# Dilated attention: statistics stored as 16-byte pieces, the softmax over dilations run inside the next pair's first pass, and 160 bytes set aside on the right

## The chip, the cores and the metric

One Trainium2 chip, of which the kernel uses one core. The metric is the device time of one execution in microseconds (us), over runs of the same program; lower is better. Everything is 32-bit floating point: a product that has to be exact is made of three matrix products over operands split into a high and a low part of type fp32r.

## The reference, cut to what matters

Two blocks over 1024 tokens of width 1024. The first runs dilated window attention beside a gated long convolution; the second (a state-space layer and a latent attention) only matters here as the rest of the time. In the first block each of 8 heads attends in three dilation groups (1, 4 and 16), and the three results are weighted by a softmax over the groups' log-denominators:

```python
for g, (window, dilation) in enumerate(DILATED_GROUPS):     # (128,1), (512,4), (2048,16)
    o_g, lse_g = dilated_window_attention(q[g], k[g], v[g], slopes, dilation, radius)
wts = softmax(stack(lses, axis=0), axis=0)
o_attn = einsum('gbsh,gbshe->bshe', wts, stack(outs, axis=0))
y_attn = o_attn.reshape(B, S, D_ATTN) * silu(g_attn)
merged = sigmoid(r_attn) * (y_attn @ w_proj_attn) + sigmoid(r_hy) * (y_hy @ w_proj_hyena)
res = DEEPNORM_ALPHA * x + gate * (merged @ w_out + b_out)
```

## The kernel before

**Who orders the work.** The code is written straight down, and a scheduler that simulates the engines decides in what order each engine takes its instructions; each engine then runs its list in that order and waits on semaphores. DMAs are issued almost all from SP, which also runs its list in order.

**The large products.** `unit()` computes 128 columns of `h @ w_in` and its like for all 1024 tokens. For each of two halves of 512 tokens it runs 8 chunks of the depth times three products on TensorE (L192): weights `wh` with `hh`, `wh` with `hl`, `wl` with `hh`. The 128x128 weight block is the stationary operand, and 512 columns of the activations are the moving one. ACT makes `wh` out of the loaded row (L177), DVE makes `wl` (L182). `hh` and `hl` are the split activations of block 1, in four tiles on the right end of SBUF, each 16 KB in every partition. The last projection of block 1 reads `mh`/`ml`, and block 2 reads `xh`/`xl`, from tiles at the same places. The first projection of the opening stage reads `hh`/`hl` too (L405), the two projections of the block's branches read `yhh`/`yhl` and `yah`/`yal`, the tail reads `xm`. The products of the long convolution (L649) have `yh`/`yl` as their moving operand.

**Where those tiles lie.** In the built program `hh0` begins at byte 196576 of each partition and `hl0` at 212960, `hh1` at 163808, `hl1` at 180192, `mh`/`ml` and `xh`/`xl` at the same numbers. All of these leave a rest of 32 when divided by 64. `yhh` begins at 42816, `yhl` at 51008, `xm0` at 113216, the convolution's `yh` and `yl` at 125760 and 131904, and these leave no rest.

**Attention.** `attention()` runs over four pairs of heads (`hp`) and three groups (`g`). A group's pass takes eight tiles of 128 queries two at a time (`tp` = 0, 2, 4, 6): scores on TensorE (L1103, L1104), bias and row minimum on DVE out of PSUM (L1105), exponential with row sum on ACT (L1108), transposes on TensorE (L1115), their copies to SBUF alternately on DVE (L999) and ACT (L1001), the product with the values (`po`, L1119), and its copies into `og` (L1129 on ACT, L1131 on DVE). Minimum and sum of each query stand in `stat`.

**Between two pairs.** After a pair's third group the statistics go to memory (`stat_d`, L1135 to L1143), two numbers of one head at a time, and come back with tokens on partitions in one DMA (`sn`, L1149). DVE and ACT work out the softmax (`mm` L1156 to `ex` L1167), the weights go out (`w_d`, L1168) and are read back spread over the 64 rows of each head (`w`, L1204), DVE (POOL for g = 1) multiplies them with `og` (L1205), DVE adds (L1207), POOL multiplies with the gate (L1210), and the result goes to memory (L1212). The scheduler moves TensorE work of the next pair, and units of other projections, into that stretch. The last pair has an ending of its own in halves of 512 tokens (L1186 to L1200), after which the merge runs, whose evacuations on DVE are `tg` (L1273).

Of the kernel before, what the change touches and what calls it, by code (L numbers as in the profile page):

```python
# [9 lines left out]
F32 = mybir.dt.float32  # L10
F32R = mybir.dt.float32r
AF = mybir.ActivationFunctionType
ALU = mybir.AluOpType
# [3 lines left out]
P = 128  # L17
S = 1024
# [142 lines left out]
def tile_pool(tc, **kw):  # L161
    return tc.tile_pool(reuse_waits="tile", **kw)
# [147 lines left out]
LAG = 0  # L310


def opening(k, cv):


# [1 line left out]

    nc, tc, A = k.nc, k.tc, k.A
    k.hh, k.hl = [], []
    for h in range(2):  # L320
        p = k.hes.enter_context(tile_pool(tc, name="hT%d" % h, bufs=1, side="right"))
        for n, to in (("hh", k.hh), ("hl", k.hl)):
            to.append(p.tile([P, KD, 512], F32R, name="%s%d" % (n, h)))
    with ExitStack() as es:
# [3 lines left out]
        xp, tp, wp = pool("xp", 8), pool("tp", 2), pool("wada", 3)  # L328
# [4 lines left out]
        xs, rows, ws, mlps = {}, {}, [], []  # L333
# [45 lines left out]
        for h in range(2):  # L379
            for n in range(FIRST):  # L380
                i = h * FIRST + n
# [592 lines left out]
def attention(k):  # L974

    nc, tc, A = k.nc, k.tc, k.A
    k.yaT = [k.dram.tile([4, P, 512], F32, name="yaT%d" % b) for b in range(2)]
    with ExitStack() as es:
# [6 lines left out]
        op = pool("og", 1)  # L985
        gp = pool("gt", 1)
        bp = pool("bias", 1)
        pt_ = pool("ptp", 4)
        st_ = pool("stat", 2)
# [6 lines left out]
        def copy(out, in_):  # L996
# [3 lines left out]
            else:  # L1000
                nc.scalar.copy(out, in_)  # L1001

        for hp in range(4):
            stat_d = k.dram.tile([3, 2, S, 2], F32, name="stat_d%d" % hp)
            w_d = k.dram.tile([3, 2, S], F32, name="w_d%d" % hp)
            og = []
            for g in range(3):
                d = (1, 4, 16)[g]
# [47 lines left out]
                tabs = []  # L1056
                for h in range(2):
                    n = 128 if g == 2 else 256
# [31 lines left out]
                for tp in range(0, 8, 2):  # L1090

                    po = ps_o.tile([P, 2, 2, P], F32, name="po", tag="po")
                    for h in range(2):
                        ps = ps_s.tile([P, 2, 256], F32, name="s%d" % h, tag="s%d" % h)
                        sb = sp.tile([P, 2, 256], F32, name="sb", tag="sb")
                        for m in range(2):
                            t = tp + m
                            a, n, off, z, cs = tiles[t]
                            qt, ks = slice(t * P, (t + 1) * P), slice(a, a + n)
                            for e, rest in ((0, z), (z + n, len(cs) * P - z - n)):  # L1100
                                if rest:
                                    nc.gpsimd.memset(sb[:, m, e : e + rest], 0.0)  # L1102
                            nc.tensor.matmul(ps[:, m, :n], qa[h][:, qt], kh[h][:, ks], start=True, stop=False)  # L1103
                            nc.tensor.matmul(ps[:, m, :n], qa[h][:, qt], kl[h][:, ks], start=False, stop=True)  # L1104
                            nc.vector.tensor_tensor_reduce(sb[:, m, z : z + n], ps[:, m, :n], tabs[h][:, off : off + n],  # L1105
                                                           -0.125, 3.0e38, op0=ALU.add, op1=ALU.min,
                                                           accum_out=stat[:, t, h, 0:1])
                            nc.scalar.activation(sb[:, m, z : z + n], sb[:, m, z : z + n], AF.Exp, scale=-1.0,  # L1108
                                                 bias=stat[:, t, h, 0:1], accum_out=stat[:, t, h, 1:2])
                        nk = len(cs)  # L1110
                        pst = ps_t.tile([P, 4, P], F32, name="pt", tag="pt")
                        pT = pt_.tile([P, 4, P], F32, name="pT", tag="pT")
                        for m in range(2):
                            for x in range(nk):
                                nc.tensor.transpose(pst[:, m * nk + x, :], sb[:, m, x * P : (x + 1) * P], k.idn)  # L1115
                        copy(pT[:, : 2 * nk], pst[:, : 2 * nk])
                        for m in range(2):
                            for x, c in enumerate(tiles[tp + m][4]):
                                nc.tensor.matmul(po[:, h, m, :], vn[:, c, :], pT[:, m * nk + x, :],  # L1119
                                                 start=(x == 0), stop=(x == nk - 1))  # L1120
                    for h in range(2):
                        hs = slice(h * 64, h * 64 + 64)
                        v, to = po[hs, h].rearrange("p m q -> p (m q)"), o[hs, tp * P : (tp + 2) * P]
                        if g:
                            rr = d // 4
                            v = v.rearrange("p (r l) -> p r l", r=rr)
                            to = o[hs].rearrange("p (l r) -> p r l", r=d)[:, tp // 2 * rr : (tp // 2 + 1) * rr]
                        if h:
                            nc.scalar.copy(to, v)  # L1129
                        else:  # L1130
                            nc.vector.tensor_copy(to, v)  # L1131
                for h in range(2):
                    dst = stat_d[g, h]
                    if g == 0:
                        nc.sync.dma_start(dst.rearrange("(t q) c -> q t c", q=P), stat[:, :, h, :])  # L1135
                    elif g == 1:
                        v = dst.rearrange("(i q r) c -> q r i c", q=P, r=4)
                        for r in range(4):
                            nc.sync.dma_start(v[:, r], stat[:, 2 * r : 2 * r + 2, h, :])
                    else:  # L1140
                        v = dst.rearrange("(l t r) c -> r l t c", r=2, t=8)
                        for r in range(2):
                            nc.sync.dma_start(v[r], stat[r * 64 : r * 64 + 64, :, h, :])  # L1143

                if (hp, g) in FILL and late:
                    r_unit(k, late.pop(0), trp)

            sn = st_.tile([P, 3, 2, 8, 2], F32, name="sn", tag="sn")
            nc.sync.dma_start(sn.rearrange("p g h j c -> p (g h) (j c)"),  # L1149
                              stat_d.rearrange("g h (p j) c -> p (g h) (j c)", j=8))  # L1150
            nm = [sn[:, g, :, :, 0] for g in range(3)]
            mm = st_.tile([P, 2, 8], F32, name="mm", tag="mm")
            ex = st_.tile([P, 3, 2, 8], F32, name="ex", tag="ex")
            zz = st_.tile([P, 2, 8], F32, name="zz", tag="zz")
            tz = st_.tile([P, 3, 2, 8], F32, name="tz", tag="tz")
            nc.vector.tensor_tensor(mm, nm[0], nm[1], op=ALU.min)  # L1156
            nc.vector.tensor_tensor(mm, mm, nm[2], op=ALU.min)
            for g in range(3):
                nc.vector.tensor_sub(ex[:, g], nm[g], mm)
            nc.scalar.activation(ex, ex, AF.Exp, scale=-1.0)  # L1160
            for g in range(3):
                nc.vector.tensor_mul(tz[:, g], ex[:, g], sn[:, g, :, :, 1])
            nc.vector.tensor_add(zz, tz[:, 0], tz[:, 1])
            nc.vector.tensor_add(zz, zz, tz[:, 2])
            nc.vector.reciprocal(zz, zz)
            for g in range(3):
                nc.vector.tensor_mul(ex[:, g], ex[:, g], zz)  # L1167
            nc.sync.dma_start(w_d.rearrange("g h (p j) -> p (g h) j", j=8), ex.rearrange("p g h j -> p (g h) j"))  # L1168

            u = UN["g_attn"] + hp  # L1170
            gt = gp.tile([P, S], F32, name="gt", tag="gt")
# [8 lines left out]
            if hp == 3:  # L1180
                for n in late:
                    r_unit(k, n, trp)
            nc.vector.scalar_tensor_tensor(gt, th, 1.0, gt, op0=ALU.add, op1=ALU.mult)
            if hp == 3:

                ws = [gp.tile([P, S], F32, name=n, tag=n) for n in ("wa", "wb")]  # L1186
# [11 lines left out]
                    nc.vector.tensor_mul(gt[:, sl], gt[:, sl], vs[0])  # L1198
                    nc.sync.dma_start(k.yaT[b][hp], gt[:, sl])
                break  # L1200
            for g in range(3):
                w = gp.tile([P, S], F32, name="w", tag="wb" if g else "wa")
                for h in range(2):
                    nc.sync.dma_start(w[h * 64 : h * 64 + 64], w_d[g, h : h + 1, :].to_broadcast([64, S]))  # L1204
                (nc.gpsimd if g == 1 else nc.vector).tensor_mul(w, w, og[g])  # L1205
                if g:
                    nc.vector.tensor_add(acc, acc, w)  # L1207
                else:
                    acc = w
            nc.gpsimd.tensor_mul(gt, gt, acc)  # L1210
            for b in range(2):
                nc.sync.dma_start(k.yaT[b][hp], gt[:, b * 512 : (b + 1) * 512])  # L1212


ON1 = ((0, 2), (0, 1, 2))
# [5 lines left out]
def merge(k):  # L1221
# [5 lines left out]
    def x2half(h):  # L1227
        p = k.x2es.enter_context(tile_pool(tc, name="x2T%d" % h, bufs=1, side="right"))
        k.x2.append([p.tile([P, KD, 512], F32R, name="x%s%d" % (n, h)) for n in "hl"])

    x2half(0)
    with ExitStack() as es, ExitStack() as em:
        def pool(name, bufs, **kw):
# [951 lines left out]
```

## Time and profile before

| | |
|---|---|
| time before, median of 3 runs | 2152.36 us (2147.53 to 2154.57) |
| the profiled execution: its own time, its span | 2153.48 us, 2151.7 us |
| mean granted TensorE clock of the span | 0.974 |
| busy: TensorE, its weight loads, DVE, ACT, POOL | 93%, 77%, 64%, 38%, 20% |
| attention lies at | about 785 to 1290 us of the span |

A row that begins with an engine and a line gives the instructions of that line: output, operands, shape and number. "PE" is TensorE, "PEld" its weight loads, "SPq" SP's issuing of DMAs. In a timeline each row is an instruction or a run of equal ones, with its start, its length, and in square brackets how long the engine stood idle ahead of it and for whom. Successive products of TensorE overlap in such rows; how fast they follow each other is read from their starts. "PEclk" is the granted clock of TensorE as a share of full speed: 1.00 is 2.4 GHz, 0.50 is 1.2 GHz.

### The profile page before, as it was taken

How to read it: one execution, taken by the hardware profiler on the slowest of the kernel's cores; microseconds unless marked ns; L12 is line 12 of the kernel's file. 1: busy time of each engine (PE TensorE's matmuls, PEld its weight loads, DVE VectorE, ACT ScalarE, POOL GpSimd, SP SyncE). 2: the span in 40 equal slices, each digit the busy share in tenths (PEclk: the TensorE clock that was granted, in tenths of full speed). 3: DMA queues.
4: the chain of work that ended last, by engine and by line, in shares of the span. 5: the costliest groups of instructions: out<-in, count | busy, mean ns of one | idle time of the engine just before them, and what ended most of it. 6: DMA issues, size and time to landing. Idle time of an engine off the chain costs nothing. (4 is left out here: it accounts for less than half of the span.)

```text
span 2151.7 us, 29886 instructions
## 1 busy us (share of the span) xinstructions
PE 2006.1 (93%) x10413; PEld 1665.3 (77%) x10413; DVE 1385.3 (64%) x2914; ACT 824.6 (38%) x1659; POOL 430.4 (20%) x448
## 2 busy tenths in 40 slices
PE   4999999999999999799897997999899989999997
PEld 3788878888887888688786875878677777788787
DVE  8987767788786234353434249585876558875685
ACT  3524333333322234444454433243423345554433
POOL 3201210231211001020201002050455233401221
PEclk9999999999999999899998999999899999999999
DMA  8236666766756473546465167363554363436351
GB/s 302 59 119 207 193 207 223 251 211 215 230 193 196 157 200 92 116 99 133 91 138 112 45 178 261 105 203 105 161 145 133 87 184 89 130 117 194 115 178 53
DMA packets 224105, 334.90 MB, mean 156 GB/s; under 512 B 65770, under 2 KB 129936, under 8 KB 223954
## 3 DMA queue, kind: packets, MB, share of 16 engines
q1 hardware_dynamic: 214016, 326.36, 50.6%
q0 software_dynamic: 1952, 4.07, 0.8%
q10 hardware_dynamic: 7986, 2.56, 0.5%
q8 instruction: 83, 1.36, 0.3%
q14 instruction: 68, 0.56, 0.1%
HBM read 251.68 MB, written 80.04 MB: 154 GB/s over the span
## 5 line engine op out<-in xcount | busy, mean ns | idle before, releaser
L192 PE MATMUL pj<-hh,wh 128*128 128x512 f32 x1104 | 441.3, 400 | 3.2 <-DVE kl L1046 2.3
L192 PE MATMUL pj<-hh,wl 128*128 128x512 f32 x1104 | 440.5, 399 | 0.1
L192 PE MATMUL pj<-hl,wh 128*128 128x512 f32 x1104 | 440.4, 399 | 0.0
L177 ACT CAST wh<-raw 128x1024 fp32r<-128x1024 f32 (+3 forms) x196 | 175.0, 897 | 377.5 <-PE pj L192 302.4
L182 DVE TENSOR_TENSOR wl<-raw,wh 128x1024 fp32r<-128x1024 f32 (+2 forms) x177 | 206.1, 1166 | 134.6 <-ACT wh L177 133.9
L192 PEld LDWEIGHTS pj<-hh,wh 128*128 128x128 f32 x1104 | 209.1, 189 | 49.6 <-issue 2.7
L192 PEld LDWEIGHTS pj<-hh,wl 128*128 128x128 f32 x1104 | 209.3, 190 | 45.5 <-DVE wl L182 0.6
L192 PEld LDWEIGHTS pj<-hl,wh 128*128 128x128 f32 x1104 | 209.2, 189 | 44.8
L1108 ACT ACTIVATE sb<-sb,stat 128x192 f32<-128x192 f32 (+2 forms) x192 | 85.5, 447 | 74.7 <-DVE stat L1105 69.4
L1119 PE MATMUL po<-pT,vn 128*128 128x128 f32 x640 | 90.7, 286 | 20.2 <-DVE pT L999 19.8
L1119 PEld LDWEIGHTS po<-pT,vn 128*128 128x128 f32 x640 | 86.1, 200 | 26.2 <-DVE pT L999 21.2
L1105 DVE CUSTOM_DVE_ANT_0 sb<-s,tb 128x192 f32<-128x192 f32 (+2 forms) x192 | 62.2, 344 | 67.9 <-PE s L1104 62.1
L192 PE MATMUL pj<-xh,wl 128*128 128x512 f32 x256 | 104.0, 406 | 1.2 <-DVE wl L182 1.2
L192 PE MATMUL pj<-xh,wh 128*128 128x512 f32 x256 | 103.4, 406 | 0.0
L192 PE MATMUL pj<-xl,wh 128*128 128x512 f32 x256 | 103.3, 404 | 0.0
L1102 POOL MEMSET sb<- 128x64 f32 x80 | 9.8, 152 | 410.3 <-PE pt L1115 364.4
L1131 DVE COPY og<-po 64x256 f32<-64x256 f32 x48 | 26.0, 541 | 86.4 <-PE po L1119 86.1
L1103 PE MATMUL s<-kh,qa 128*128 128x192 f32 (+2 forms) x192 | 60.5, 324 | 16.5 <-DVE stat L1105 15.8
L806 POOL TENSOR_TENSOR zz<-zz,t 128x256 f32<-128x256 f32 x32 | 35.4, 1107 | 182.7 <-DVE t L802 142.2
L1115 PE MATMUL pt<-idn,sb 128*128 128x128 f32 x320 | 63.9, 289 | 3.4 <-ACT sb L1108 2.1
L494 DVE TENSOR_TENSOR bt<-bt 128x256 f32<-128x256 f32 x176 | 63.5, 418 | 0.4
L192 PEld LDWEIGHTS pj<-xh,wl 128*128 128x128 f32 x256 | 48.9, 191 | 13.5 <-DVE wl L182 1.7
(602 smaller groups left out, 4630.4 us busy)
## 6 DMA issues: line engine op xcount, KB each, us to landing
raw<-in_w_in_dram SPq DMA_DIRECT2D x92, 512.0 KB, 3.7
k_fw<-k_fw SPq DMA_DIRECT2D x56, 384.0 KB, 3.8
qkv<-tr SPq DMA_DIRECT2D x80, 256.0 KB, 2.8
raw<-in_w_out_dram SPq DMA_DIRECT2D x32, 512.0 KB, 3.6
k_iv<-k_iv SPq DMA_DIRECT2D x28, 384.0 KB, 4.7
row<-in_w_ada_dram SPq DMA_DIRECT2D x16, 512.0 KB, 6.4
dc<-in_k_decay_dram SPq DMA_DIRECT2D x64, 128.0 KB, 3.5
spec<-sp SPq DMA_DIRECT2D x32, 256.0 KB, 5.3
```

Of the source, the lines that this page charges most:

```text
L177: nc.scalar.copy(hi, src)
L182: (nc.vector if lo_eng == "dve" else nc.gpsimd).tensor_sub(lo, src, f(hi))
L192: nc.tensor.matmul(ps, a, b, start=(i == 0), stop=(i == n - 1))
L494: self.nc.vector.tensor_tensor(out, a, b, op=op)
L806: nc.gpsimd.tensor_sub(zz[:, 0], zz[:, 0], t2[:, 1])
L1102: nc.gpsimd.memset(sb[:, m, e : e + rest], 0.0)
L1103: nc.tensor.matmul(ps[:, m, :n], qa[h][:, qt], kh[h][:, ks], start=True, stop=False)
L1105: nc.vector.tensor_tensor_reduce(sb[:, m, z : z + n], ps[:, m, :n], tabs[h][:, off : off + n], -0.125, 3.0e38, op0=ALU.add, op1=ALU.min, a ...
L1108: nc.scalar.activation(sb[:, m, z : z + n], sb[:, m, z : z + n], AF.Exp, scale=-1.0, bias=stat[:, t, h, 0:1], accum_out=stat[:, t, h, 1:2])
L1115: nc.tensor.transpose(pst[:, m * nk + x, :], sb[:, m, x * P : (x + 1) * P], k.idn)
L1119: nc.tensor.matmul(po[:, h, m, :], vn[:, c, :], pT[:, m * nk + x, :], start=(x == 0), stop=(x == nk - 1))
L1131: nc.vector.tensor_copy(to, v)
```

## The change

Three things are edited.

1. `stat_d` gets a layout with both heads side by side for each token (`[3, S, 2, 2]`), so that a piece written for a query is 16 bytes long where it was 8, and each store carries both heads: 28 stores where there were 56. `sn` then reads pieces of 128 bytes where they were 64.
2. What stood between two pairs becomes a generator, `combined()`, whose steps run inside the next pair's pass over g = 0: the load of `sn` at `tp` = 2; softmax, `w_d` and the loads of two of the three weights at `tp` = 4; the multiplications, the third load, the sums and the stores at `tp` = 6. `issue_after(dve.ins)` and `issue_after(act.ins)` let the scheduler place such a step only behind the last score reduction and the last exponential of that `tp`. The last pair runs the first two steps at once and keeps its own ending.
3. `pad()` takes a tile of 40 numbers (160 bytes) on the right ahead of `hh`/`hl`, and again ahead of `xh`/`xl`. In the built program these tiles, and `mh`/`ml`, begin 160 bytes lower: 196416, 212800, 163648, 180032, which leave no rest when divided by 64. No other moving operand of 512 columns changes its place.

The number of instructions is otherwise the same on each engine.

```diff
+def pad(k, es):
+    es.enter_context(tile_pool(k.tc, name="pad", bufs=1, side="right")).tile([P, 40], F32, name="pad")
...
     k.hh, k.hl = [], []
+    pad(k, k.hes)
...
+        def combined(hp, stat_d, w_d, og):
+            sn = st_.tile([P, 3, 8, 2, 2], F32, name="sn", tag="sn")
+            nc.sync.dma_start(sn.rearrange("p g j h c -> p g (j h c)"),
+                              stat_d.rearrange("g (p j) h c -> p g (j h c)", j=8))
+            yield
...
+            nc.vector.tensor_tensor(mm, nm[0], nm[1], op=ALU.min)
...
+            for g in range(3):
+                nc.vector.tensor_mul(ex[:, g], ex[:, g], zz)
+            nc.sync.dma_start(w_d.rearrange("g h (p j) -> p (g h) j", j=8), ex.rearrange("p g h j -> p (g h) j"))
+            if hp == 3:
+                yield
+            ws = {}
...
+            load(0)
+            load(1)
+            yield
+            for g in range(3):
+                if g == 2:
+                    load(2)
+                (nc.gpsimd if g == 1 else nc.vector).tensor_mul(ws[g], ws[g], og[g])
+                if g:
+                    nc.vector.tensor_add(ws[0], ws[0], ws[g])
+            gt = gts[hp]
+            nc.gpsimd.tensor_mul(gt, gt, ws[0])
...
-            stat_d = k.dram.tile([3, 2, S, 2], F32, name="stat_d%d" % hp)
+            stat_d = k.dram.tile([3, S, 2, 2], F32, name="stat_d%d" % hp)
...
+                    if g == 0 and tp in (2, 4, 6):
+                        with tc.issue_after(dve.ins), tc.issue_after(act.ins):
+                            next(pending, None)
...
-                        for r in range(2):
-                            nc.sync.dma_start(v[r], stat[r * 64 : r * 64 + 64, :, h, :])
+                    for r in range(2):
+                        nc.sync.dma_start(v[r], sv[r * 64 : r * 64 + 64])
...
+            pending = combined(hp, stat_d, w_d, og)
+            if hp == 3:
+                next(pending)
+                next(pending)
...
+    pad(k, k.x2es)
     x2half(0)
```

Three places show how the order moves. The line numbers of the changed file differ: L1105 is L1163 there, L1156 to L1167 are L1023 to L1034, L1205 and L1207 are L1051 and L1053.

**First place: the start of the softmax between the first and the second pair.** On DVE before, where `s_8700` and `s_8721` are scores of the second pair's `tp` = 2, `s_8745` and `s_8766` those of its `tp` = 4:

```order
L1105 ISA sb,stat<-s_8721,tb_8630 128x256
L1105 ISA stat 128x1
L1105 ISA sb,stat<-s_8745,tb_8628 128x256
L1105 ISA stat 128x1
L1156 TENSOR_TENSOR mm<-sn 128x16
L1157 TENSOR_TENSOR mm<-mm,sn 128x16
L1159 TENSOR_TENSOR ex<-sn,mm 128x16 x3
L999 COPY pT<-pt 128x512
```

and of the change, where `s_8679` stands for `tp` = 2, and `s_8705` and `s_8726` for `tp` = 4:

```order
L1163 ISA sb,stat<-s_8679,tb_8588 128x256
L1163 ISA stat 128x1
L1163 ISA sb,stat<-s_8705,tb_8586 128x256
L1163 ISA stat 128x1
L1005 COPY pT<-pt 128x512
L1163 ISA sb,stat<-s_8726,tb_8588 128x256
L1163 ISA stat 128x1
L1163 ISA sb,stat<-s_8705,tb_8586 128x256
L1163 ISA stat 128x1
L1189 COPY og_8609<-po 64x256
L1163 ISA sb,stat<-s_8726,tb_8588 128x256
L1163 ISA stat 128x1
L1023 TENSOR_TENSOR mm<-sn 128x16
```

The first instruction that needs `sn` stood behind one reduction of `tp` = 4; now it stands behind all four, a copy of `pT` and one of `og`. On SP before, at the same place:

```order
L1143 DMA stat_d_7599<-stat 512x1x2 x4
L297 DMA raw<-in_w_in_dram 128x1024
L1031 DMA qa_8901<-qkv_6546 64x1024
L1149 DMA sn<-stat_d_7599 128x6x16
```

and of the change:

```order
L1203 DMA stat_d_7603<-stat 512x1x4 x2
L1089 DMA qa_8897<-qkv_6550 64x1024 x2
L297 DMA raw<-in_w_in_dram 128x1024
L1014 DMA sn<-stat_d_7603 128x3x32
```

Four stores became two; `sn` still stands behind them with two or three loads between.

**Second place: the multiplications with the weights, same pair.** On DVE before, where `og_7644` is the first pair's result of g = 0 and `ex` was finished 24 rows earlier:

```order
L1046 SCALAR_TENSOR_TENSOR qa_9144<-pj,cols,qa_9144 64x16x32
L1205 TENSOR_TENSOR w<-w,og_7644 128x1024
L1207 TENSOR_TENSOR w<-w 128x1024
L1105 ISA sb,stat<-s_8963,tb_8922 128x192
L1105 ISA stat 128x1
L999 COPY vn<-pt 128x512
```

and of the change:

```order
L1034 TENSOR_TENSOR ex<-ex,zz 128x16 x3
L1189 COPY og_8609<-po 64x256
L1005 COPY vn<-pt 128x512
L1051 TENSOR_TENSOR w<-w,og_7648 128x1024
L1163 ISA sb,stat<-s_8985,tb_8916 128x192
L1163 ISA stat 128x1
L1163 ISA sb,stat<-s_9008,tb_8918 128x192
L1163 ISA stat 128x1
L1104 SCALAR_TENSOR_TENSOR kl_9139<-pj,cols,kh_9137 64x16x32
L1104 SCALAR_TENSOR_TENSOR kl_9140<-pj,cols,kh_9138 64x16x32
L1053 TENSOR_TENSOR w<-w 128x1024
L1005 COPY pT<-pt 128x512
```

The first multiplication now stands three rows behind the end of the softmax, and the first sum is ahead of a copy of `pT`. On TensorE of the change 21, 19 and 20 products of L192, with 32 products of the attention between them, stand ahead of the `po` that reads that `pT`. After it come eight transposes, four scores and 23 products of L192, and then a `po` behind the third multiplication.

**Third place: the end of the last pair.** On DVE before, where `wa`, `wb` and `pT` hold the weights and `tg` are the merge's evacuations:

```order
L1167 TENSOR_TENSOR ex<-ex,zz 128x16 x2
L182 TENSOR_TENSOR wl<-raw,wh 128x1024
L1167 TENSOR_TENSOR ex<-ex,zz 128x16
L1273 SCALAR_TENSOR_TENSOR tg_12212<-tg_12212,pj 128x512
L1273 SCALAR_TENSOR_TENSOR tg_12228<-tg_12228,pj 128x512
L182 TENSOR_TENSOR wl<-raw,wh 128x1024
L1273 SCALAR_TENSOR_TENSOR tg_12250<-tg_12250,pj 128x512
L1273 SCALAR_TENSOR_TENSOR tg_12266<-tg_12266,pj 128x512
L1195 TENSOR_TENSOR wa<-wa,og_10665 128x512
```

and of the change:

```order
L1034 TENSOR_TENSOR ex<-ex,zz 128x16 x3
L182 TENSOR_TENSOR yhl<-yt,yhh 128x512
L182 TENSOR_TENSOR yal<-yt,yah 128x512 x2
L1189 COPY og_11350<-po 64x4x64
L182 TENSOR_TENSOR yal<-yt,yah 128x512
L1238 TENSOR_TENSOR wa<-wa,og_10609 128x512
L1238 TENSOR_TENSOR wb<-wb,og_10934 128x512
L182 TENSOR_TENSOR wl<-raw,wh 128x1024
```

The multiplications stood behind four `tg`; now they stand ahead of all of them.

## Rows read from the trace of the kernel before

**Rows 1.** The page, busy time of each engine in the span.

```profile
PE 2006.1 (93%) x10413; PEld 1665.3 (77%) x10413; DVE 1385.3 (64%) x2914; ACT 824.6 (38%) x1659; POOL 430.4 (20%) x448
```

**Rows 2.** Waits of PE, 780 to 1280: us in total, times, longest us.

```profile
PE po L1119 <- DVE pT L999: 19.8, 3, 11.2
PE s L1103 <- DVE stat L1105: 15.8, 6, 6.2
```

**Rows 3.** Waits of PE, 1125 to 1185, the third change of pairs.

```profile
PE po L1119 <- DVE pT L999: 8.2, 1, 8.2
```

**Rows 4.** Waits of DVE, 780 to 1280, same columns.

```profile
DVE mm L1156 <- DMA sn<-stat_d: 29.7, 3, 12.8
DVE w L1205 <- DMA w<-w_d: 17.7, 6, 6.6
DVE w L1207 <- POOL w L1205: 12.7, 3, 7.9
```

**Rows 5.** Timeline of SP at the first change of pairs.

```profile
891.16 2.80 SPq L1143 DMA_DIRECT2D stat_d<-stat  x4
...
904.20 0.38 SPq L1149 DMA_DIRECT2D sn<-stat_d  x1
```

**Rows 6.** Timeline of DVE at the first change of pairs.

```profile
910.48 0.17 DVE L1156 TENSOR_TENSOR mm<-sn 128x16 f32<-128x16 f32 x1 [12.78 <-DMA sn<-stat_d]
...
913.73 0.35 DVE L1167 TENSOR_TENSOR ex<-ex,zz 128x16 f32<-128x16 f32 x3
...
925.24 1.23 DVE L1205 TENSOR_TENSOR w<-w,og 128x1024 f32<-128x1024 f32 x1 [0.74 <-DMA w<-w_d]
934.34 1.23 DVE L1207 TENSOR_TENSOR w<-w 128x1024 f32<-128x1024 f32 x1 [7.88 <-POOL w L1205]
```

**Rows 7.** Windows behind four stalls: length, PE, PEld, DVE, ACT, POOL busy, PEclk, DMA.

```profile
911.90:917.30 5.40, 5.40 (x25) 5.40 (x26) 3.62 (x19) 3.02 (x10) 0.23 (x2) 0.51 1.02 246
1028.77:1033.30 4.53, 4.53 (x21) 4.53 (x22) 2.87 (x16) 2.98 (x10) 0.23 (x2) 0.50 0.55 157
1142.35:1146.00 3.65, 3.65 (x17) 3.65 (x18) 2.57 (x17) 2.19 (x7) 0.14 (x2) 0.51 1.03 236
936.02:941.00 4.98, 4.98 (x16) 4.20 (x17) 2.26 (x5) 2.92 (x7) 0.24 (x2) 0.50 0.45 106
```

**Rows 8.** DMA issues, 780 to 1290: number, KB each, median us to landing.

```profile
stat_d<-stat SPq DMA_DIRECT2D x32, 2.0 KB, 1.9
stat_d<-stat SPq DMA_DIRECT2D x16, 4.0 KB, 8.0
```

**Rows 9.** Timeline of PE, two runs of products of L192.

```profile
1248.13 0.40 PE L192 MATMUL pj<-hh,wl 128*128 128x512 f32 x1
...
1252.12 0.40 PE L192 MATMUL pj<-hl,wh 128*128 128x512 f32 x1
...
1265.68 0.39 PE L192 MATMUL pj<-yhh,wh 128*128 128x512 f32 x1
...
1270.91 0.39 PE L192 MATMUL pj<-yhh,wl 128*128 128x512 f32 x1
```

**Rows 10.** Groups of PE by line: number, busy us, mean ns of one.

```profile
L192 PE MATMUL pj<-hh,wh 128*128 128x512 f32 x1104 | 441.3, 400 | 3.2 <-DVE kl L1046 2.3
L192 PE MATMUL pj<-xh,wh 128*128 128x512 f32 x256 | 103.4, 406 | 0.0
L192 PE MATMUL pj<-mh,wh 128*128 128x512 f32 x128 | 52.3, 411 | 0.8 <-ACT wh L177 0.4 <-ACT mh L1291 0.3
```

**Rows 11.** Timeline of PE, three products of the long convolution.

```profile
501.12 0.40 PE L649 MATMUL hx<-yh,k_fw 128*128 128x512 f32 x1
...
501.58 0.39 PE L649 MATMUL hx<-yh,k_fw 128*128 128x512 f32 x1
```

**Rows 12.** Waits of PE, 1255 to 1312, columns as in the second group.

```profile
PE psr L1403 <- DVE rows L1400: 5.8, 1, 5.8
PE pj L192 <- DVE tg L1273: 2.8, 1, 2.8
```

More of the change, by code (lines that the diff above doesn't have):

```diff
@@ L1001, in copy, with load @@
                 nc.scalar.copy(out, in_)
+        def combined(hp, stat_d, w_d, og):
[3 more added lines that the diff above has]
+            yield
+            sn = sn.rearrange("p g j h c -> p g h j c")
+            nm = [sn[:, g, :, :, 0] for g in range(3)]
+            mm = st_.tile([P, 2, 8], F32, name="mm", tag="mm")
+            ex = st_.tile([P, 3, 2, 8], F32, name="ex", tag="ex")
+            zz = st_.tile([P, 2, 8], F32, name="zz", tag="zz")
+            tz = st_.tile([P, 3, 2, 8], F32, name="tz", tag="tz")
+            nc.vector.tensor_tensor(mm, nm[0], nm[1], op=ALU.min)
+            nc.vector.tensor_tensor(mm, mm, nm[2], op=ALU.min)
+            for g in range(3):
+                nc.vector.tensor_sub(ex[:, g], nm[g], mm)
+            nc.scalar.activation(ex, ex, AF.Exp, scale=-1.0)
+            for g in range(3):
+                nc.vector.tensor_mul(tz[:, g], ex[:, g], sn[:, g, :, :, 1])
+            nc.vector.tensor_add(zz, tz[:, 0], tz[:, 1])
+            nc.vector.tensor_add(zz, zz, tz[:, 2])
+            nc.vector.reciprocal(zz, zz)
+            for g in range(3):
+                nc.vector.tensor_mul(ex[:, g], ex[:, g], zz)
[3 more added lines that the diff above has]
+            ws = {}
+            def load(g):
+                ws[g] = gp.tile([P, S], F32, name="w", tag="wb" if g else "wa")
+                for h in range(2):
+                    nc.sync.dma_start(ws[g][h * 64 : h * 64 + 64], w_d[g, h : h + 1, :].to_broadcast([64, S]))
+            load(0)
+            load(1)
+            yield
+            for g in range(3):
+                if g == 2:
[5 more added lines that the diff above has]
+            nc.gpsimd.tensor_mul(gt, gt, ws[0])
+            for b in range(2):
+                nc.sync.dma_start(k.yaT[b][hp], gt[:, b * 512 : (b + 1) * 512])
+            yield
@@ L1003, in attention @@
+        gts, pending = {}, iter(())
         for hp in range(4):
-            stat_d = k.dram.tile([3, 2, S, 2], F32, name="stat_d%d" % hp)
+            stat_d = k.dram.tile([3, S, 2, 2], F32, name="stat_d%d" % hp)
             w_d = k.dram.tile([3, 2, S], F32, name="w_d%d" % hp)
@@ L1104, in attention @@
                             nc.tensor.matmul(ps[:, m, :n], qa[h][:, qt], kl[h][:, ks], start=False, stop=True)
-                            nc.vector.tensor_tensor_reduce(sb[:, m, z : z + n], ps[:, m, :n], tabs[h][:, off : off + n],
+                            dve = nc.vector.tensor_tensor_reduce(sb[:, m, z : z + n], ps[:, m, :n], tabs[h][:, off : off + n],
                                                            -0.125, 3.0e38, op0=ALU.add, op1=ALU.min,
                                                            accum_out=stat[:, t, h, 0:1])
-                            nc.scalar.activation(sb[:, m, z : z + n], sb[:, m, z : z + n], AF.Exp, scale=-1.0,
+                            act = nc.scalar.activation(sb[:, m, z : z + n], sb[:, m, z : z + n], AF.Exp, scale=-1.0,
                                                  bias=stat[:, t, h, 0:1], accum_out=stat[:, t, h, 1:2])
@@ L1131, in attention @@
                             nc.vector.tensor_copy(to, v)
[L1132 to L1141, printed above, removed]
-                        for r in range(2):
-                            nc.sync.dma_start(v[r], stat[r * 64 : r * 64 + 64, :, h, :])
+                    if g == 0 and tp in (2, 4, 6):
+                        with tc.issue_after(dve.ins), tc.issue_after(act.ins):
+                            next(pending, None)
@@ new lines, in attention @@
+                dst, sv = stat_d[g].rearrange("s h c -> s (h c)"), stat.rearrange("q t h c -> q t (h c)")
+                if g == 0:
+                    nc.sync.dma_start(dst.rearrange("(t q) c -> q t c", q=P), sv)
+                elif g == 1:
+                    v = dst.rearrange("(i q r) c -> q r i c", q=P, r=4)
+                    for r in range(4):
+                        nc.sync.dma_start(v[:, r], sv[:, 2 * r : 2 * r + 2])
+                else:
+                    v = dst.rearrange("(l t r) c -> r l t c", r=2, t=8)
+                    for r in range(2):
+                        nc.sync.dma_start(v[r], sv[r * 64 : r * 64 + 64])
@@ L1145, in attention @@
                 if (hp, g) in FILL and late:
                     r_unit(k, late.pop(0), trp)
[L1148 to L1168, printed above, removed]
+            pending = combined(hp, stat_d, w_d, og)
+            if hp == 3:
+                next(pending)
+                next(pending)
@@ L1183, in attention @@
             nc.vector.scalar_tensor_tensor(gt, th, 1.0, gt, op0=ALU.add, op1=ALU.mult)
+            gts[hp] = gt
             if hp == 3:
@@ L1200, in attention @@
                 break
[L1201 to L1212, printed above, removed]
 ON1 = ((0, 2), (0, 1, 2))
```

## The prediction

> **What bounds the kernel now.** I read the page first. TensorE is busy for 2006.1 of 2151.7 us, no other engine for more than 64% [rows 1]. So the time is the products themselves, at the pace at which they follow each other, plus the 145.6 us in which TensorE stands. A change that only takes work off DVE, ACT or a queue gives nothing; it must either let TensorE stand less or let its products follow faster. The change reaches for both.
>
> Then I read the waits over attention. TensorE stands 19.8 us ahead of `po` and 15.8 us ahead of the scores, both for DVE [rows 2]. What DVE waits for is in its own waits: 29.7 us in three waits for `sn`, 17.7 us for the weights `w`, 12.7 us for POOL's product [rows 4]. These lie at the three changes of pairs. The timeline of the first shows how: four stores of the statistics are issued from 891.16, `sn` is issued at 904.20 [rows 5], DVE has it at 910.48 after 12.78 us [rows 6], and TensorE, whose `po` needs a copy that stands behind it on DVE, has stood for 11.2 us by then. The windows show what a stall costs beyond itself: behind it the granted clock is 0.50 of full, 1.2 instead of 2.4 GHz, for some 4 to 5 us [rows 7].
>
> **What the wait for the statistics costs today.** The idle of TensorE is 11.2 us at the first change, 6.2 at the second [rows 2] and 8.2 at the third [rows 3], 25.6 us. The first three windows behind them are 5.40, 4.53 and 3.65 us of products at half clock [rows 7], 13.6 us, half of which is lost: 6.8. Together **32.4 us**. The rest of rows 2, 19.8 + 15.8 - 25.6 = 10.0 us, belongs mostly to the weights; one window behind such a stall is 4.98 us at half clock [rows 7], 2.5 lost; three like it make 7.5. That is **17.5 us** for the weights.
>
> **Statistics in 16-byte pieces, and the softmax later.** A store of 256 pieces lands after 1.9 us; the four of 512 pieces, 2048 in one go, land after 8.0 [rows 8]. If pieces set this, one costs (8.0 - 1.9) / 1792 = 3.4 ns, and 1024 pieces of 16 bytes land after 1.9 + 768 x 3.4 ns = 4.5 us. If bytes set it, 8.0 stays. The trace has no 16-byte store; I take 4.5, since 16 bytes are much nearer to 8 than to any row that moves at a rate of bytes. The issuing of two stores takes 1.4 us where four took 2.80 [rows 5]. So `sn` is issued 1.4 + 3.5 = 4.9 us sooner, and with half its pieces (384 for 768) it may land another 1.3 sooner (384 x 3.4 ns). On DVE its first reader now stands behind three more reductions and two copies, about 2.5 to 3.5 us of work, which also hands TensorE what it lacked. Of 12.8 us there remain 12.8 - 4.9 - 1.3 - 3 = 3.6; of the two others, 16.9 in all, nothing. I take 4 us of loss with the half clock, so **-28.5**. Ends: -32.4 if all is hidden; -10 if bytes set the stores, when only the 3 us of shift count at each change.
>
> **The weights.** This is where the moved stall can reappear. Today the softmax ends at 913.73 + 0.35 = 914.08, and the first multiplication comes at 925.24, 11.2 us later; it waits only 0.74, since 24 rows of other work lie between [rows 6]. In the change three rows lie between, so DVE stands there about 10 us at each change of pairs. The path itself (`w_d` out, `w` in) is not shortened. Behind it stand reductions, the split `kl`, the sum (which waits for POOL) and the `pT` copy that TensorE's next `po` needs. What covers it is TensorE's list: 60 products of L192 and 32 small ones. At 0.235 us [rows 9] the 60 take 14.1 us; the small ones at half of 5.40 / 25 us [rows 7] take 3.5: 17.6 us. The sum ran 934.34 - 913.73 = 20.6 us behind the softmax at the first change [rows 6], because POOL's wait was 7.9; at the others it was 12.7 - 7.9 = 4.8 for two [rows 4], so about 11.2 + 1.2 + 2.4 = 14.8. With 1.8 us for the sum and copy, `pT` is ready after 22.4 or 16.6: a stall of 4.8 us once (7.3 with the half clock), none twice. Then the third weight, loaded only behind the sum, holds DVE again (longest wait so far 6.6, rows 4) with 23 products, 5.4 us, and 12 small ones, 1.3, as cover, against 6.6 and some 6 us of work queued behind: about 3 us idle and 1.5 of half clock at each. Sum 7.3 + 13.5 = 20.8, against 17.5: **+3**. Ends: -17.5 if the cover always holds, and +25 if both stalls come at the first change's size (14.3 each, 43 in all).
>
> **The 160 bytes.** A run of `hh` and `hl` products starts at 1248.13 and its eighteenth at 1252.12: 17 steps of 234.7 ns. Sixteen us later, at the same clock and with the same kind of weights, `yhh` and `yhl` take 23 steps from 1265.68 to 1270.91: 227.4 ns [rows 9]. What differs is the moving operand's place: a rest of 32 to a multiple of 64 bytes for the slow run, none for the fast. The shift takes `hh`/`hl`, `mh`/`ml` and `xh`/`xl` to no rest: 3 x (1104 + 128 + 256) = 4464 products of L192 [rows 10]. 7.3 ns each is 32.6 us; nothing if the place is not the cause. The convolution's products speak against a clean rule: they have no rest and yet step at 230 ns, two in 0.46 us [rows 11]. I take 6 ns, since products in short runs, or ahead of another wait, don't give it all back: **-26.8**.
>
> The page "SBUF — State Buffer" of the Trainium skill, section "Specifications (TRN2)", says that reads go by lines of 16 bytes. Both places are multiples of 16, and by that rule the shift changes nothing and the sum would be 2127; but the rule puts both runs of rows 9 at one pace, and they are 7.3 ns apart.
>
> **The ending.** With the last pair the multiplications come ahead of the merge's `tg` evacuations, so DVE waits for weights (some 10 us, as above) before it frees TensorE's accumulators: up to +6 if the products on hand run out. In exchange the attention ends sooner, and the 5.8 us that TensorE stands for `psr` behind it, and the 2.8 for `tg` [rows 12], shrink: down to -6. I take **0**. The 28 stores less free SP of up to 20 us of issuing, at 0.7 us each [rows 5], all but 1.4 us at each change of pairs off the path.
>
> **Sum.** 2153.5 - 28.5 + 3 - 26.8 = 2101.2 for the profiled execution, which stands 1.1 us over the median: **2100 us**.
>
> **Rivals.**
> 1. *The offset does nothing*; the stalls go. Rows 11 and the skill's line speak for it, rows 9 against. 2100 + 26.8 = 2127 us.
> 2. *The stall only changes its name.* Bytes set the stores (-10), or the weights' wait takes the upper end (+25) while the pace gains: 2153.5 - 10 + 3 - 26.8 = 2120, or 2153.5 - 28.5 + 25 - 26.8 = 2123; both, 2142. For it speaks that the chain from statistics to sum is no shorter than its DMAs; against it the 60 products.
> 3. *Slower: DVE's list is held by the weights with no cover.* If TensorE needs something behind the first multiplication already after 40 of the products (9.4 us), a change of pairs costs 10 at the first weight, 9 at the sum and 11 at the third, 30 - 9.4, with 5 us of half clock 25 us; 75 - 17.5 = +57.5, so 2153.5 - 28.5 + 57.5 - 26.8 = 2156 us, or 2183 with no gain in pace. It decides from a loss of 17.5 + 55.3 = 73 us in three changes on, 24 each, or 15 each without the pace. Against it: the scores behind the first weight have their reductions done ahead of it in the order.
>
> **Chances.** The forecast 0.56, with its own range 2080 to 2118; rival 1 0.15; rival 2 0.17; rival 3 0.08, of which 0.06 slower. What is left, 0.04, is that the pace and the stalls both stay as they are. About 0.3%, 6.5 us, is what a measurement of this kernel can tell from no change. Faster by more than that: forecast, rivals 1 and 2, 0.88. Same: 0.06. Slower: 0.06. The range from 2074 to 2134 takes in the forecast, rival 1 and most of rival 2, and leaves out rival 3.
>
> **What would show it.** In the profile of the change: `hh` products that step at 227 to 229 ns; DVE's waits for `sn` under 6 us in all, and TensorE's waits for DVE in attention from 35.6 us to under 18; waits for `w` that grow from 17.7 to 35 us or more on DVE without TensorE's following; stores of 16-byte pieces that land after 4 to 5 us. Wrong, if the steps stay at 234, if 16-byte stores take 8 us, or if windows of half clock stand behind the first multiplication of every change of pairs.

## The result, and the profile after

The change takes 2100.49 us (median of 4 runs, 2098.30 to 2102.66) against 2153.47 us: ratio 0.9766, 95% interval 0.9734 to 0.9798: about 50 us less by the ratio, 53 between the medians. The profiled run has 2102.66 us, its span 2100.6, at a mean clock of 0.978.

The page's busy line, beside [rows 1]:

```profile
PE 1974.5 (94%) x10413; PEld 1655.7 (79%) x10413; DVE 1385.3 (66%) x2914; ACT 824.1 (39%) x1659; POOL 431.9 (21%) x448
```

TensorE is busy 31.6 us less for the same number of products; the other engines do what they did. One cause is the pace. The timeline of TensorE, a run of products of L192 that answers to the first pair in [rows 9]:

```profile
600.18 0.40 PE L192 MATMUL pj<-hl,wh 128*128 128x512 f32 x1
...
605.88 0.39 PE L192 MATMUL pj<-hh,wl 128*128 128x512 f32 x1
```

These are 25 steps of 228.0 ns, where `hh` and `hl` stepped at 234.7. Then the waits of TensorE over attention, 780 to 1280 (total, times, longest), beside [rows 2]:

```profile
PE s L1162 <- DMA kl<-qkv: 7.4, 7, 1.9
PE pj L192 <- DVE tg L1305: 7.0, 3, 4.4
PE s L1161 <- DVE stat L1163: 4.0, 4, 1.2
PE s L1161 <- DMA kh<-qkv: 0.9, 1, 0.9
...
PE s L1161 <- DMA kl<-qkv: 0.7, 1, 0.7
```

The wait of `po` for DVE, 19.8 us before, is gone, and that of the scores for DVE fell from 15.8 to 4.0. New at the changes of pairs is the wait for `kl` and `kh`, loads of the next group: 8.2 us of these rows lie at the three changes, where before there was none. The `tg` lie behind the last pair, which the same window now takes in, since the attention ends at about 1258. The waits of DVE, beside [rows 4]:

```profile
DVE w L1051 <- DMA w<-w_d: 9.7, 4, 3.4
DVE mm L1023 <- DMA sn<-stat_d: 5.3, 3, 2.6
DVE w L1053 <- POOL w L1051: 2.9, 3, 1.5
```

All three fell: `sn` from 29.7 (2.7 us of the 5.3 are left at the three changes, the rest is the last pair's), the weights from 17.7, POOL's product from 12.7. SP's timeline at the first change of pairs, beside [rows 5], and DVE's, beside [rows 6]:

```profile
881.78 1.23 SPq L1203 DMA_DIRECT2D stat_d<-stat  x2
888.69 0.38 SPq L1014 DMA_DIRECT2D sn<-stat_d  x1
```

```profile
907.38 0.34 DVE L1034 TENSOR_TENSOR ex<-ex,zz 128x16 f32<-128x16 f32 x3
913.48 0.42 DVE L1189 COPY og<-po 64x256 f32<-64x256 f32 x1 [5.75 <-PE po L1177]
914.63 1.23 DVE L1051 TENSOR_TENSOR w<-w,og 128x1024 f32<-128x1024 f32 x1
...
919.38 1.23 DVE L1053 TENSOR_TENSOR w<-w 128x1024 f32<-128x1024 f32 x1 [0.67 <-POOL w L1051]
...
925.30 1.23 DVE L1051 TENSOR_TENSOR w<-w,og 128x1024 f32<-128x1024 f32 x1 [3.43 <-DMA w<-w_d]
```

From the first store to `sn` it is 6.9 us where it was 13.0. From the end of the softmax to the first multiplication it is 6.9 us where it was 11.2. DVE did not wait for the weights in that time: it stood 5.75 us for TensorE, whose `po` the copy into `og` between them reads, and the multiplication came without a wait. At the other two changes it is 6.7 and 7.0 us, with 0.3 us or less of waiting for `w`. What still stands at a change of pairs shows in the windows of the second one (length, busy time of the engines, PEclk, DMA share, GB/s):

```profile
1002.00:1008.00 6.00, 2.41 (x16) 1.92 (x16) 1.80 (x5) 3.24 (x9) 0.00 (x0) 0.96 1.02 254
1008.00:1014.00 6.00, 5.04 (x15) 3.56 (x14) 3.99 (x15) 2.49 (x8) 0.46 (x4) 0.50 0.25 51
```

TensorE stands 3.6 us in the first window, with the DMA engines full, and runs at half clock in the second. To have one number for this, I add over windows of 1 us the time that TensorE is not busy and its busy time times (1 - granted clock). From 785 to 1310 us that is 53.6 + 18.1 = 71.7 us before, and from 775 to 1258 us 22.8 + 11.2 = 34.0 us after.

### The profile page after: what moved, and what is told of

Read it like the earlier page. It is cut to its first block, busy times and chain, and to the rows that moved or that the text cites. A ratio compares the mean times of both kernels' runs of the same rounds, so it can differ in the third digit from the quotient of the medians.

```text
span 2100.6 us, 29821 instructions
## 1 busy us (share of the span) xinstructions
PE 1974.5 (94%) x10413; PEld 1655.7 (79%) x10413; DVE 1385.3 (66%) x2914; ACT 824.1 (39%) x1659; POOL 431.9 (21%) x448
## 5 line engine op out<-in xcount | busy, mean ns | idle before, releaser
L192 PE MATMUL pj<-hh,wh 128*128 128x512 f32 x1104 | 436.7, 396 | 1.4 <-DVE tr L961 0.8
L192 PE MATMUL pj<-hl,wh 128*128 128x512 f32 x1104 | 436.4, 395 | 0.0
L192 PE MATMUL pj<-hh,wl 128*128 128x512 f32 x1104 | 434.8, 394 | 0.1
L177 ACT CAST wh<-raw 128x1024 fp32r<-128x1024 f32 (+2 forms) x196 | 175.0, 897 | 360.6 <-PE pj L192 289.4
L192 PEld LDWEIGHTS pj<-hh,wh 128*128 128x128 f32 x1104 | 209.0, 189 | 44.1 <-PE pj L192 1.7
L192 PEld LDWEIGHTS pj<-hh,wl 128*128 128x128 f32 x1104 | 209.0, 189 | 40.4 <-DVE wl L182 0.6
L192 PEld LDWEIGHTS pj<-hl,wh 128*128 128x128 f32 x1104 | 209.2, 189 | 39.5
L1163 DVE CUSTOM_DVE_ANT_0 sb<-s,tb 128x192 f32<-128x192 f32 (+2 forms) x192 | 62.6, 344 | 103.9 <-PE s L1162 85.4
L192 PE MATMUL pj<-xh,wl 128*128 128x512 f32 x256 | 102.1, 399 | 1.3 <-DVE wl L182 1.3
L192 PE MATMUL pj<-xl,wh 128*128 128x512 f32 x256 | 102.1, 399 | 0.2 <-DVE xl L182 0.2
L192 PE MATMUL pj<-xh,wh 128*128 128x512 f32 x256 | 101.3, 398 | 0.0
L1177 PE MATMUL po<-pT,vn 128*128 128x128 f32 x640 | 84.1, 277 | 1.1 <-ACT pT L1007 0.8
L1177 PEld LDWEIGHTS po<-pT,vn 128*128 128x128 f32 x640 | 79.7, 191 | 5.7 <-ACT pT L1007 1.9
L1162 PE MATMUL s<-kl,qa 128*128 128x192 f32 (+2 forms) x192 | 53.2, 285 | 8.1 <-DMA kl<-qkv 8.1
L1173 PE MATMUL pt<-idn,sb 128*128 128x128 f32 x320 | 58.4, 280 | 0.9 <-DVE vn L1005 0.3
```

Source lines behind the costliest of these rows:

```text
L177: nc.scalar.copy(hi, src)
L192: nc.tensor.matmul(ps, a, b, start=(i == 0), stop=(i == n - 1))
L1163: dve = nc.vector.tensor_tensor_reduce(sb[:, m, z : z + n], ps[:, m, :n], tabs[h][:, off : off + n], -0.125, 3.0e38, op0=ALU.add, op1=ALU.min,
```

## The experiments

Each ran beside the kernel before on the same chip; ratios are to it, with 95% intervals.

**The offset alone, and the change without it.** The first is the kernel before with

```diff
+    pad(k, k.hes)
...
+    pad(k, k.x2es)
```

and the second the change without these lines. The order on every engine is that of before, or of the change; only addresses differ.

> Before with the 160 bytes alone; every engine's order is that of before. Theory A (the place of the moving operand sets the pace, and the pace is on the path nearly everywhere, as the prediction had it): products with hh, hl, xh, xl, mh, ml step at 227 to 229 ns, and the time falls by about 27 us, to 2127. Theory B (the pace changes, but other waits take up half of it, as idle and half clock in the profile after suggest): the same steps, but only about 13 us, 2140. Rival (the offset does nothing, all came from the stalls): steps at 234, 2153.

> The change without the 160 bytes; every engine's order is that of the change. Theory A: steps at 234 ns, stalls as in the change, 2127. Theory B (idle and half clock in attention fell by 38 us, from 71.7 to 34.0): 2115. Rival (the offset does nothing): 2100.

The offset alone: 2135.85 us against 2150.95, ratio 0.9934 (0.9922 to 0.9947), 14 us. The change without it: 2114.81, ratio 0.9838 (0.9822 to 0.9855), 35 us. Theory B holds. A third pair that differs by the offset alone, the pieces without and with it (below), agrees: ratios 0.9861 and 0.9790, 15 us. The mean step of all `hh` products is 228.4 ns with the offset and 233.9 without. 4464 of them at 5.6 ns are 25 us, of which 11 do not arrive. Block 2 shows some of it; the products with `xh`, first and last start, of the run with the offset alone:

```profile
L192 PE MATMUL pj<-xh,wh x256: 387/389/628, 1463.9 to 1727.8; 128*128 128x512 f32 x128
```

This stage takes 263.9 us; before it was 262.7, from 1483.2 to 1745.9, although its 768 products should have given 4.3 us. One pair says little here: in the two others the offset makes the stage shorter, 264.7 to 262.4 us in the change and 263.2 to 261.2 us with the pieces. The mean of the three is 1 us of the 4.3. The idle and half-clock time of the whole span, added as above, is 193 us in this run and 183 before. So a run of products ends sooner, and TensorE meets the next wait sooner and stands there; which waits these are was not followed one by one.

**Which offset.** The change with a `pad()` of 16, 8 or 104 numbers in place of 40, and one with 32 numbers on the right and 8 on the left, ahead of the weights:

```diff
-    ...tile([P, 40], F32, name="pad")
+    ...tile([P, 16], F32, name="pad")     # then 8, 104, and 32 with:
+        es.enter_context(tile_pool(tc, name="padl", bufs=1)).tile([P, 8], F32, name="padl")
```

> The change with 64 bytes set aside in place of 160: the operands move, but keep the rest of 32 to a multiple of 64. If the rest is the cause, steps at 234 ns and the time of the change without the bytes (2115 to 2127). If any move of place helps, 228 ns and 2100.

> The change with 32 bytes set aside in place of 160: no rest to 64, as in the change, at other places to 512 or 128. If the rest to 64 is the cause, 228 ns and 2100. If 160 bytes are special (a place relative to the weights, or to a larger block), 234 ns or something between, and over 2105.

> The change with 416 bytes in place of 160: hh, xh, mh then begin at 64 past a multiple of 512, the weights wh, wl as always at 320 past one, 256 apart. Theory (what counts is that the operand and the weights lie at the same place within 256 bytes): steps of 228 ns and the time of the change, 2100. Rival (32 bytes set aside gave 232.5 ns, so any place that is not 320 past a multiple of 512 is slow): 232 ns or more, 2107 or more.

> The change with 128 bytes on the right in place of 160 and 32 bytes on the left ahead of the weights: operands and weights both begin at 352 past a multiple of 512, and so do yhh and yhl. Theory (their places relative to each other count): 228 ns for hh and for yhh, 2100. Rival (the operand's own place counts, 64 past a multiple of 256): 232 to 234 ns for both, over 2110.

| bytes right, left | place of `hh`, of `wh` (rest to 512) | apart, rest to 256 | mean step of `hh`, ns | ratio |
|---|---|---|---|---|
| 0, 0 (second run) | 480, 320 | 160 | 233.9 | 0.9838 (0.9822 to 0.9855) |
| 64, 0 | 416, 320 | 96 | 233.7 | 0.9829 (0.9813 to 0.9844) |
| 32, 0 | 448, 320 | 128 | 232.5 | 0.9803 (0.9786 to 0.9820) |
| 160, 0 (the change) | 320, 320 | 0 | 228.4 | 0.9766 (0.9734 to 0.9798) |
| 416, 0 | 64, 320 | 0 | 228.4 | 0.9791 (0.9769 to 0.9812) |
| 128, 32 | 352, 352 | 0 | 228.4 | 0.9766 (0.9741 to 0.9791) |

The step is the mean of all pairs of successive products whose starts are under 260 ns apart. Runs of the timeline for 32 bytes, and for 128 and 32:

```profile
601.46 0.39 PE L192 MATMUL pj<-hl,wh 128*128 128x512 f32 x1
...
605.87 0.40 PE L192 MATMUL pj<-hh,wl 128*128 128x512 f32 x1
```

```profile
597.58 0.40 PE L192 MATMUL pj<-hl,wh 128*128 128x512 f32 x1
...
604.86 0.39 PE L192 MATMUL pj<-hh,wh 128*128 128x512 f32 x1
```

The first is 19 steps of 232.1 ns, the second 32 of 227.5. So a move by itself gives nothing (64 bytes), and no rest to 64 is not the rule (32 bytes, 232.5). In all three fast layouts the operand and the weights lie at the same place within 256 bytes, and the last one shows that it is their relative place: there both have a rest of 32 to 64. The same run moves the weights against the tiles that it leaves alone: `u`, at 480, was 160 apart and stepped at 234.0; now it is 128 apart and steps at 232.6, as `hh` did at 128.

**The pieces alone, and the later softmax alone.** No offset in either. The first is the kernel before with the layout `[3, S, 2, 2]`, its 28 stores and its `sn`; the second has the generator, but the stores and the layout of before:

```diff
-            stat_d = k.dram.tile([3, S, 2, 2], F32, name="stat_d%d" % hp)
+            stat_d = k.dram.tile([3, 2, S, 2], F32, name="stat_d%d" % hp)
```

> Before with the 16-byte pieces and the 128-byte reads alone; softmax and sums where they were, no offset. Theory A (pieces set the stores, as the prediction had it): sn is issued about 5 us sooner after the stores, DVE's waits for it fall from 29.7 to about 11 us, and with the half clock the time falls by about 20 us, to 2131. Theory B (the stores' time is set by their number and the queue, little by their pieces; what helped was the place of the softmax): under 10 us, over 2141.

> Before with the softmax and the sums run inside the next pair's first pass, but with 8-byte pieces and no offset. Theory A: only about 12 us of the 36 that came from pieces and place together, 2139. Theory B (the place hands TensorE so much cover that the statistics' path matters little): 28 us or more, 2123 or less.

The pieces alone: 2112.27 against 2143.64 us, ratio 0.9861 (0.9834 to 0.9888), 30 us. The later softmax alone: 2141.01, ratio 0.9992 (0.9979 to 1.0005), nothing. The waits of the pieces' run over 780 to 1280, then those of the later softmax:

```profile
DVE mm L1156 <- DMA sn<-stat_d: 15.8, 4, 5.7
PE po L1119 <- DVE pT L999: 7.7, 2, 4.2
PE s L1103 <- DVE stat L1105: 4.9, 4, 2.2
```

```profile
DVE mm L1021 <- DMA sn<-stat_d: 20.7, 4, 8.1
PE s L1159 <- DVE stat L1161: 28.3, 8, 7.5
PE s L1160 <- DMA kl<-qkv: 7.6, 6, 2.1
```

With short pieces DVE's wait halves and TensorE's falls from 35.6 to 12.6. With the softmax later and the old pieces DVE still stands 20.7 us for `sn`, and TensorE's wait only changes its name: no longer the copy of `pT`, but the scores, held by reductions that stand behind the softmax on DVE. Theory A holds, and more than holds, though DVE's wait fell to 15.8 us and not to 11: the 35 us are the pieces' within the intervals, and the place adds nothing that can be told (some 5 us would still fit the intervals). With short pieces the place trades one loss for another. TensorE's waits in the change without the offset, beside those of the pieces' run:

```profile
PE s L1161 <- DMA kl<-qkv: 6.6, 5, 1.8
PE s L1160 <- DVE stat L1162: 4.4, 5, 1.1
PE s L1160 <- DMA kh<-qkv: 1.6, 2, 0.9
```

For DVE 12.6 us became 4.4, but 6.9 us of the waits for `kl` and `kh` lie at the three changes, where the pieces' run has none. By the sum used above, idle and half clock over attention, the two runs are level: 26.0 + 5.1 = 31.1 us with the pieces alone (785 to 1270) and 20.4 + 10.8 = 31.2 us with the later place as well (783 to 1268). Before it was 71.7, and with the later softmax alone 65.5 (782 to 1300).

The pieces' run also shortens the load `sn`. From its issue to the reader on DVE, which waited for it each time, the load took 6.3, 3.9 and 4.3 us at the three changes before and 5.2, 3.4 and 4.1 us in this run. So 1 us or less of each change is the load's; from the first store to `sn` it is 6.6 us at the first change and 7.2 at the third, 13.0 at both before.

**Both without the later softmax.** The pieces' run with the offset.

> Before with the 16-byte pieces and the 160 bytes, softmax and sums where they were. Theory (the place of the softmax gives nothing, as its run alone showed): as fast as the whole change, ratio 0.977 to 0.980, some 2100 to 2106. Rival (the place pays once the pieces are short): slower than the whole change by 6 us or more.

2099.43 against 2145.75 us, ratio 0.9790 (0.9773 to 0.9807): the interval overlaps that of the whole change.

**Pieces or stores.** The pieces' run with every store cut in two, for the third group

```diff
-                        nc.sync.dma_start(v[r], sv[r * 64 : r * 64 + 64])
+                        for x in range(0, 8, 4):
+                            nc.sync.dma_start(v[r][:, x : x + 4], sv[r * 64 : r * 64 + 64, x : x + 4])
```

> The run with the 16-byte pieces alone, but each store cut in two, 56 as before with the pieces of 16 bytes. Theory (the number of pieces counts): as with 28 stores, ratio about 0.986, 2113 to 2120. Rival (the number of stores counts, each with its issue of 0.6 us and its own landing): at least half of the gain gone, ratio 0.993 or more.

2107.05 us, ratio 0.9829 (0.9810 to 0.9848): nothing of the gain is lost with 56 stores. It isn't a clean doubling, as SP's timeline shows:

```profile
864.05 1.31 SPq L1146 DMA_DIRECT2D stat_d<-stat  x2
...
888.25 1.28 SPq L1146 DMA_DIRECT2D stat_d<-stat  x2
...
893.59 0.38 SPq L1152 DMA_DIRECT2D sn<-stat_d  x1
```

Half of the stores leaves 24 us sooner, while the group runs, and only the second half is on the path: 5.3 us to `sn`. So the number of stores in all does not matter here. On the path it is two in this run and in the pieces' run, and four before; that number was never changed without the pieces. The run shows one thing more. Both pairs of stores carry the same 256 pieces each, but the early ones land after 2.0 and 2.2 us and the late ones after 5.1 and 4.6. What differs in the windows (columns as above) is the DMA share, 0.11 for the early pair and 0.99 for the late one, around which SP issues the loads `kh`, `qa` and `raw`:

```profile
864.05:866.95 2.90, 2.90 (x14) 2.35 (x13) 0.00 (x0) 0.69 (x1) 0.00 (x0) 1.00 0.11 11
888.25:893.59 5.34, 5.02 (x39) 4.38 (x39) 5.10 (x17) 5.27 (x16) 0.00 (x0) 1.00 0.99 182
```

**What still holds the changes of pairs.** Two tries on top of the whole change: `sn` issued from POOL (`nc.gpsimd.dma_start`), and the third group's stores cut as above.

> The whole change with sn issued from POOL in place of SP, so that the loads of kh and kl of the next group no longer stand behind its wait for the stores. Theory (in the change TensorE's 8 us for kl and kh at the changes of pairs, and the half clock behind, come from SP standing at sn): these waits go, 10 us or more faster than the change, 2090 or less. Rival (the loads then fill the DMA engines and sn lands later): DVE's waits for sn grow from 5.3 us to over 12 and the time stays at 2095 to 2105.

> The whole change with the third group's stores cut in halves of four tiles, so that the first half can leave while the group still runs and only 512 pieces are left behind its end. Theory (what still holds TensorE at the changes of pairs is kl and kh, whose loads stand on SP behind sn, which waits for those stores): sn is issued some 2 us sooner after the last store, TensorE's 8 us for kl and kh shrink to about 4 with less half clock behind, 5 to 8 us faster than the change, ratio 0.973 to 0.975. Rival (loads of 2 MB behind sn are bound by the DMA engines, not by SP): the ratio of the change, 0.976 to 0.977.

`sn` from POOL: 2105.54 us, ratio 0.9823 (0.9794 to 0.9851), not faster than the change. The rival holds, its time just over the upper end that it named; DVE's wait, TensorE's, and the landing (KB each, median us):

```profile
DVE mm L1023 <- DMA sn<-stat_d: 20.7, 4, 6.8
PE s L1161 <- DVE stat L1163: 12.9, 5, 6.1
sn<-stat_d POOLq DMA_DIRECT2D x4, 48.0 KB, 8.3
```

The waits for `kl` go, and `sn` takes longer: 5.1 to 9.8 us from its issue to its landing, where in the change its reader on DVE had it 1.9 to 6.0 us after its issue.

The cut stores: 2088.14 against 2149.02 us, ratio 0.9717 (0.9704 to 0.9731), the fastest here, some 10 us below the change; the two intervals just clear each other. Its waits:

```profile
DVE mm L1023 <- DMA sn<-stat_d: 1.1, 1, 1.1
PE s L1162 <- DMA kl<-qkv: 5.3, 4, 2.1
PE pj L192 <- DVE tg L1306: 3.4, 2, 2.3
PE s L1161 <- DVE stat L1163: 2.3, 3, 1.4
```

The size came as expected, the way only in part. At the three changes `kl` and `kh` went from 8.2 to 4.9 us, near the 4 expected, but the time lost to half clock stayed, 11.0 us after 11.2; as much came from `tg` behind the last pair, 7.0 to 3.4 us, which was not expected, and 1.7 us from the scores.

## Why the prediction was right

The sum was 2100 us and the result 2100.49. The two causes are those that were forecast, but that the numbers meet within 1 us is luck: the stalls gave 35 us where the sum had 25.5, the offset 14 where it had 26.8, and the two errors cancelled.

- **Statistics (-28.5).** The mechanism held: stores to `sn` 6.9 us (predicted 13.0 - 4.9 = 8.1), DVE's waits for `sn` 5.3 (predicted under 6). The landing of one store didn't: the third group's land after 7.2 us, where 4.5 was worked out and four smaller ones took 8.0 [rows 8]:

```profile
stat_d<-stat SPq DMA_DIRECT2D x8, 8.0 KB, 7.2
```

  What fell is the time from the first store to the landing of the last. The 3.4 ns per piece failed as a price. It compares stores that leave in mid-group with stores that leave beside the next group's loads, and the run with 56 stores has stores of one size at 2.0 to 2.6 us in the one place and 4.6 to 5.3 in the other. So part of what was put on the pieces probably belongs to these loads, and that the term came as near as it did is in part luck. What I put on the place of the softmax (3 us at each change, "which also hands TensorE what it lacked") was wrong as a gain of its own: that run gave nothing. I had counted as cover what is also work queued ahead of the softmax; behind it the scores wait instead.
- **The weights (+3).** The failed step is "The path itself (`w_d` out, `w` in) is not shortened", and with it the 10 us that DVE was to stand at the first weight. The path took at most 7.0 us at each change, where it took 7.6 to 12.0 before. DVE stood 0.3 us or less for the first weight, since in the rows ahead of it it stood 5.6 to 5.9 us for TensorE. Its waits for `w`, forecast to grow to 35 us, fell to 9.7, nearly all at the third weight, and those for POOL's product to 2.9. So no stall moved there. Together statistics and weights were put at -25.5; the run without the offset has -35.

  The path is shorter with the later place, as the runs with one edit each show. The first load of `w` waits for `w_d` to land. It comes 2.0 to 2.3 us after `w_d` is issued at the three changes of the change, and 2.0 to 2.1 with the later softmax alone; the DMA share of these stretches is 0.19 to 0.27, the loads of the next group being through by then. With the pieces alone it is 3.7 to 6.3 us at a share of 0.70 to 0.78. Before it was 6.3 and 7.0 us at 0.76 and 0.78, and 2.8 once, at 0.17.

  The working of the third weight does not come out either: 6.6 + 6 us against 5.4 + 1.3 of cover leaves 5.9 idle, not 3. TensorE stood for none of it.
- **What is late next** was sought at the weights and lies at `kl` and `kh`, 8.2 us in the change. SP issues them behind `sn`, whose wait holds them; and when it doesn't, they hold `sn`.
- **The 160 bytes (-26.8).** The gain per product was near, 5.6 ns in the mean of all where 7.3 was read from two runs of products and 6 taken; the time was -14. Mis-sized was what other waits take back: I let 18% of 7.3 ns go for them, and of the 25 us that the shorter steps make, 11 went. The rule behind it, a rest to 64 bytes, fell with the 32-byte run; 160 bytes fit that rule and the true one alike. The line of 16 bytes in the Trainium skill, "SBUF — State Buffer", section "Specifications (TRN2)", would have all six layouts at one pace; they differ by 5.5 ns, so it can't be the whole of what a product's reads cost.
- **The ending (0).** TensorE's waits there changed names and stayed near in size: `psr` 5.8 and `tg` 2.8 us before [rows 12], and 7.0 us for `tg` after, the row shown with TensorE's waits above.

Rival 3 stayed away, since the stall behind the first multiplication never came: in the change no `po` of TensorE waits for a `pT` copy of DVE.

## What to carry to other kernels

Look at the pieces of a small store, and at the loads that leave beside it: 8-byte pieces made 16 bytes long, and half as many, on a path that an engine in order waits on, gave 30 us of 2150, and sending half of them early gave 10 more. Moving a waiting step later in an engine's order gave nothing here by itself, since what stands behind it is also waited for; look at what TensorE needs next from that engine. And a faster pace of the products is not the number of products times the step: count what the next waits take back before it goes into a sum.

## What the runs showed of the hardware that was not expected

The step between successive 128x512 products depends on where the moving operand lies relative to the weights: 227.5 to 228.4 ns when both begin at the same place within 256 bytes, 232.5 at 128 bytes apart, 233.7 at 96 and 233.9 at 160. It is the same for two absolute places of the weights. The rule is not complete: the long convolution's products lie 0 apart too, and their steps average 229 to 233 ns by operand, before and after; the 230 ns of [rows 11] is one such reading. Why they do, and why the relative place counts at all, stays open.
